# Two middle groups of 256 features made one of 512 in the first GEMM of a hybrid decoder layer

## The chip, the cores and the metric

The kernel runs on one core of one Trainium2 chip. The metric is the device time of one launch in microseconds (us). All inputs lie in HBM and the result is written to HBM.

## The reference, cut to what matters

One decoder layer: the input x (512 tokens, 2048 features, float32) is normalised, scaled and shifted by a conditioning vector, and multiplied by a wide matrix w_in. Behind it come a convolution branch, an attention branch, gates and two more projections, none of which the change touches.

```python
c_act = jax.nn.silu(c)                                   # (1, 2048)
mod = c_act @ w_ada + b_ada                              # w_ada: 2048 x 6144
shift, scale, gate = jnp.split(mod, 3, axis=-1)
h = rms_norm(x, g_pre) * (1.0 + scale) + shift           # 512 x 2048
p = h @ w_in                                             # w_in: 2048 x 11264
cv, cg, cz, q, k, v, az, m_conv, m_attn = split(p)       # cv, cg: 1024 columns each
u = cv * sigmoid(cg)
```

The columns of `mod` are dot products over all 2048 entries of c_act. A feature of h can therefore be formed only when its whole column of shift and its whole column of scale have been read, 2 x 2048 float32 numbers of w_ada per feature.

## The kernel before

**Precision.** Every float32 operand of a large product is split into two float32r parts, hi and lo (`split`, lines 141 to 151: the cast hi on ScalarE at line 145, the rest lo = src - hi on VectorE at line 146). A product is then three matmuls, hi*hi, hi*lo, lo*hi (`mm3`, line 167), each with a moving operand of 512 tokens.

**The first GEMM** computes cv and cg, 2048 output columns, which are 16 blocks of 128. It is the only product that runs while h is still being made. The 2048 features of h, the contraction, are 16 tiles of 128 (index k), and they are taken in the groups of `GROUPS`. An entry is (first feature, width, npe). For each group two generators exist:

- `ada(c0, width, npe)`, lines 287 to 339, makes h for the group. It loads w_ada in chunks of 512 KB (two DMAs of 256 KB on SP's queue, line 281, into a ring of AR = 6 buffers, tile `ada`). There are 16 steps kk, one for each 128 rows of w_ada. Of these, npe go to TensorE: two matmuls each (shift and scale) into 32 rows of a PSUM bank, tile `pa`, line 302, so that the matmuls of two such steps use four different column strips of the array. The others go to VectorE, one multiply-add over both halves, tile `acc`, lines 305 and 307. At the end the sums over 128 partitions are taken by matmuls with one or two output columns (tile `pm`). Where npe is 16, one matmul for each block of 128 features does it (line 318). Where npe is 0, two per block (line 324). Where npe lies between, four per block (lines 323 and 324), after VectorE has copied `pa` to `accp` (line 314). Three small VectorE operations give shift and scale, tiles `sh` and `scl` (lines 328 to 330). ScalarE then forms h (`hf`, line 335), and h is split into `hp`.
- `conv_gemm(k0, nk)`, lines 348 to 377, multiplies the nk tiles of the group by w_in. With nk = 2 it works in four steps of four output blocks, with nk = 4 in eight steps of two output blocks. Each step loads weights in blocks of 512 KB (`wr_c`, line 155, three buffers), splits them (`wh_c`, `wl_c`) and accumulates in PSUM tiles `pc` (four banks). For the first group ScalarE copies the results to `part` (line 367). For every later group VectorE adds each of the 16 PSUM tiles to its `part` (line 369). After the last group, `part` becomes u (lines 375 to 377).

**Order.** Lines 398 to 408 join the conv_gemm of group i with the ada of group i + 1, in program order, in proportion 4 or 8 steps of the one to `ST[i]` steps of the other:

```python
for i, (c0, width, _) in enumerate(GROUPS[:-1]):
    k0, nk = c0 // P, width // P
    conv, group = conv_gemm(k0, nk), ada(*GROUPS[i + 1])
    ...
    interleave((conv, 8 if nk == 4 else 4), (group, ST[i]), *([(rest, 8)] if i == 0 else []))
...
interleave((conv_gemm(KT - 4, 4), 8))
```

A step counts as issued when its share is the smallest. The compiler's planner then orders the instructions of each engine by this program order and by its own estimate of when each is ready. Each engine and SP's queue runs its list strictly in order.

Before the change the seven groups are 128, 128, 256, 256, 256, 512 and 512 features wide. The group that starts at 512 has all 16 sums on TensorE, that at 768 all on VectorE, that at 1024 half on each, and that at 1536 all on VectorE. After the first GEMM come v, q, k, attention, the gates and the projections.

Of the kernel before, what the change touches and what calls it, by code (L numbers as in the profile page):

```python
# [41 lines left out]
SKIP = 4  # L42
RES = 8
AR = 6
ST = (3, 10, 10, 10, 13, 10)

GROUPS = ((0, 128, 16), (128, 128, 16), (256, 256, 0), (512, 256, 16), (768, 256, 0),
          (1024, 512, 8), (1536, 512, 0))


@with_exitstack
def hybrid_trunk(ctx: ExitStack, tc: tile.TileContext, x, c, w_ada, b_ada, g_pre, g_post, w_in,
# [17 lines left out]
    def page(name, dt=F32):  # L70
        return pp.tile([P, S], dt, tag="pg", name=name)
# [105 lines left out]
    def interleave(*gens):  # L177

        gens = [[g, n, 0] for g, n in gens]
        while gens:  # L180
            g = min(gens, key=lambda e: (e[2] + 1) / e[1])
            g[2] += 1
            if next(g[0], StopIteration) is StopIteration:
                gens.remove(g)


    with tc.tile_pool(name="ps0", bufs=1, space=PSUM) as ps0, tc.tile_pool(name="ap", bufs=1) as ap:
# [70 lines left out]
        def norm_x(ks):  # L258
            for k in ks:
                nc.vector.tensor_tensor(xn[k], pxt[k], rsb, op=ALU.mult)  # L260

        def turn_norm(ks):
            for k in ks:
                turn((k,), range(NT))
                norm_x((k,))
                yield
# [81 lines left out]
        def conv_gemm(k0, nk):  # L348
            first, last = k0 == 0, k0 + nk == KT
            wk = min(nk, 4)  # L350
            nf = min(4, 8 // wk)
            for g in range(8 // nf):
                for a, c0 in ((0, C_CV), (1, C_CG)):
                    ps = [gbank(f"pc_{k0}_{g}_{a}_{f}") for f in range(nf)]
                    for q0 in range(k0, k0 + nk, wk):
                        key = (q0, g, a)
                        whi, wlo = early.pop(key) if key in early else conv_wsplit(q0, wk, g, nf, a, c0)
                        for f in range(nf):
                            fs = slice(f * P, (f + 1) * P)
                            for k in range(wk):  # L360
                                last_mm[0] = mm3(ps[f], (whi[:, k, fs], wlo[:, k, fs]), h[q0 + k],
                                                 q0 + k == k0, q0 + k == k0 + nk - 1)
                    for f in range(nf):
                        i = a * 8 + g * nf + f
                        if first:
                            part[i] = page(f"part_{i}")
                            nc.scalar.copy(part[i], ps[f])
                        else:
                            nc.vector.tensor_tensor(part[i], ps[f], part[i], op=ALU.add)  # L369
                    yield  # L370
                if last:
                    for f in range(nf):
                        i = g * nf + f
                        th = part[8 + i]
                        nc.scalar.activation(th, th, AF.Tanh, scale=0.5)
                        u[i] = page(f"u_{i}")
                        nc.vector.scalar_tensor_tensor(u[i], th, 1.0, part[i], op0=ALU.add, op1=ALU.mult)

        with tc.manual_schedule(engines={mybir.EngineType.PE, mybir.EngineType.Activation, mybir.EngineType.DVE}):
# [6 lines left out]
            norm_x(range(4))  # L386
            group = ada(*GROUPS[0])
            next(group)
# [8 lines left out]
        rest = turn_norm(range(8, KT))  # L397
# [3 lines that stand above are left out]
            if i == 0:  # L401
# [3 lines left out]
                with tc.issue_after(last_mm[0].ins):  # L405
                    for _ in range(2):
                        next(group)
            interleave((conv, 8 if nk == 4 else 4), (group, ST[i]), *([(rest, 8)] if i == 0 else []))
        cwrow = page("cwrow")
# [862 lines left out]
```

## Time and profile before

| what | us |
|---|---|
| median of 3 runs | 1429.47 |
| the 3 runs | 1425.40, 1429.47, 1429.83 |
| the profiled execution, its own time | 1427.9 |
| its span in the profile | 1426.1 |
| around the span (1427.9 - 1426.1) | 1.8 |

All rows below come from the profiled execution. Times in them are us from the start of the span unless marked ns. PE is TensorE, PEld its weight loads, DVE VectorE, ACT ScalarE, SP the queue that issues the transfers. An x behind a name is a number of recorded instructions. A float32 matmul, as in `pa` and `pm`, leaves two records, a float32r matmul one. An arrow and a name behind an idle time tell what ended it.

### The profile page before, as it was taken

To read this page: it belongs to the slowest core of one execution; us is meant where nothing else is said; L and a number is where in the kernel's file an instruction comes from. 1 tells how busy PE (TensorE), PEld (TensorE's weight loads), DVE (VectorE), ACT (ScalarE), POOL (GpSimd) and SP (SyncE) were. 2 spreads that over 40 slices of the span, in tenths; PEclk is the share of its full clock that TensorE was granted. 3 is DMA by queue.
4 is the path that set the end of the run, shared out by engine and by line. 5 is a ranking of instruction groups with operands and counts; after the bars stand their busy time and mean duration, and the time that the engine had idled before them with its cause. 6 is when DMAs were issued, how large, how long until landed. Compare 5 with 4: busy or idle time off the path is not lost.

```text
span 1426.1 us, 20678 instructions
## 1 busy us (share of the span) xinstructions
PE 1379.1 (97%) x7903; PEld 1171.8 (82%) x7903; DVE 1158.4 (81%) x1882; ACT 560.9 (39%) x907; POOL 59.6 (4%) x103
## 2 busy tenths in 40 slices
PE   5999999999999999999999999999999999989995
PEld 4676788887767877788999999999998888868784
DVE  6997975988888887588997788898966848897876
ACT  3421332223343244434544444444445313344443
POOL 0000000000000000000000000111000211010000
PEclk9999999999999999999999999999999999999998
DMA  9889733331322422233545556756569855546588
GB/s 300 288 285 308 232 117 102 118 130 63 102 83 69 131 67 82 74 126 134 200 161 188 176 171 193 255 196 200 171 204 345 301 182 194 198 122 211 171 238 262
DMA packets 178757, 254.89 MB, mean 179 GB/s; under 512 B 10065, under 2 KB 120994, under 8 KB 178274
## 3 DMA queue, kind: packets, MB, share of 16 engines
q1 hardware_dynamic: 169778, 227.61, 48.0%
q0 software_dynamic: 8880, 25.96, 6.9%
q8 instruction: 62, 1.02, 0.3%
q14 instruction: 37, 0.30, 0.1%
HBM read 221.29 MB, written 30.15 MB: 176 GB/s over the span
## 4 chain that ended last, share of the span: by engine, by line
PE 81%; DVE 10%; DMA 4%; issue 2%; ACT 2%; SPq 1%; DVEq 0%; ACTq 0%
PE pc L167 11%; PE py_ya L167 6%; PE pv L167 6%; PE pg_k L167 6%; PE pg_az L167 5%; PE pg_q L167 5%; PE x_ma L167 5%; PE x_mc L167 5%; PE z_mc L167 3%; PE z_ma L167 3%; PE y_ma L167 3%; PE y_mc L167 3%; PE x_cz L167 2%; PE oy L167 2%; DMA ga<-scratch_mc 2%
## 5 line engine op out<-in xcount | busy, mean ns | idle before, releaser
L500 DVE SCALAR_TENSOR_TENSOR cacc<-u,cw,cacc 128x511 f32<-128x511 f32 (+14 forms) x240 | 164.5, 729 | 0.0
L167 PE MATMUL pc<-hp,wh_c 128*128 128x512 f32 x512 | 160.2, 398 | 3.1 <-DVE part L369 1.2
L167 PEld LDWEIGHTS pc<-hp,wh_c 128*128 128x128 f32 x512 | 95.9, 190 | 29.1 <-issue 2.7
L167 PE MATMUL pc<-hp,wl_c 128*128 128x512 f32 x256 | 99.3, 397 | 2.1 <-DVE wl_c L146 2.1
L369 DVE TENSOR_TENSOR part<-pc,part 128x512 f32<-128x512 f32 x96 | 64.8, 688 | 25.3 <-PE pc L167 24.8
L167 PE MATMUL pv<-wh_v,hp 128*128 128x512 f32 x256 | 82.9, 398 | 0.9 <-DVE part L369 0.9
L167 PE MATMUL pg_q<-hp,wh_q 128*128 128x512 f32 x256 | 82.7, 399 | 0.0
L167 PE MATMUL pg_az<-hp,wh_az 128*128 128x512 f32 x256 | 81.5, 396 | 0.0
L167 PE MATMUL pg_k<-hp,wh_k 128*128 128x512 f32 x256 | 80.2, 393 | 0.0
L167 PE MATMUL py_ya<-ya,wh_ya 128*128 128x512 f32 x256 | 78.9, 390 | 0.0
L145 ACT CAST wh_c<-wr_c 128x1024 fp32r<-128x1024 f32 (+1 forms) x36 | 34.2, 956 | 104.1 <-PE pc L167 45.2
L167 PEld LDWEIGHTS pc<-hp,wl_c 128*128 128x128 f32 x256 | 48.5, 190 | 14.1 <-DVE wl_c L146 3.3
L167 PEld LDWEIGHTS pv<-wh_v,hp 128*128 128x128 f32 x256 | 47.8, 188 | 14.2 <-issue 4.5
L167 PEld LDWEIGHTS pg_az<-hp,wh_az 128*128 128x128 f32 x256 | 47.8, 188 | 11.9 <-issue 2.7
L167 PEld LDWEIGHTS pg_q<-hp,wh_q 128*128 128x128 f32 x256 | 47.3, 188 | 12.3 <-issue 2.8
L167 PEld LDWEIGHTS py_ya<-ya,wh_ya 128*128 128x128 f32 x256 | 48.0, 188 | 9.8
L652 POOL DMA_DIRECT2D adag<-in_w_ada_dram x64 | 34.2, 537 | 516.1 <-ACT oh L145 309.4
L167 PEld LDWEIGHTS pg_k<-hp,wh_k 128*128 128x128 f32 x256 | 48.0, 188 | 9.4
L307 DVE SCALAR_TENSOR_TENSOR acc<-ada,cact,acc 128x512 f32<-128x512 f32 (+1 forms) x52 | 50.5, 972 | 1.6 <-DMA ada<-in_w_ada_dram 1.4
L167 PE MATMUL py_yc<-ych,wh_yc 128*128 128x512 f32 x128 | 50.8, 397 | 0.3 <-DVE ga L957 0.3
L167 PE MATMUL pg_k<-hp,wl_k 128*128 128x512 f32 x128 | 51.1, 399 | 0.0
L167 PE MATMUL pv<-wl_v,hp 128*128 128x512 f32 x128 | 50.6, 396 | 0.0
(413 smaller groups left out, 3997.6 us busy)
## 6 DMA issues: line engine op xcount, KB each, us to landing
ada<-in_w_ada_dram SPq DMA_DIRECT2D x128, 256.0 KB, 5.4
wr_ma<-in_w_in_dram SPq DMA_DIRECT2D x16, 1024.0 KB
wr_mc<-in_w_in_dram SPq DMA_DIRECT2D x16, 1024.0 KB, 5.3
adag<-in_w_ada_dram POOLq DMA_DIRECT2D x64, 256.0 KB, 4.5
wr_c<-in_w_in_dram SPq DMA_DIRECT2D x28, 512.0 KB, 6.0
wr_v<-in_w_in_dram SPq DMA_DIRECT2D x8, 1024.0 KB, 6.8
wr_q<-in_w_in_dram SPq DMA_DIRECT2D x8, 1024.0 KB, 5.0
wr_k<-in_w_in_dram SPq DMA_DIRECT2D x8, 1024.0 KB, 5.3
```

The source lines that it names most:

```text
L145: nc.scalar.copy(hi, src)
L167: mm = nc.tensor.matmul(ps, a[p], b[q], start=start and i == 0, stop=stop and i == 2, skip_group_check=more)
L307: nc.vector.scalar_tensor_tensor(acc, raw[:, kk - k0, :, :], cact[:, kk:kk + 1], acc, op0=ALU.mult, op1=ALU.add)
L369: nc.vector.tensor_tensor(part[i], ps[f], part[i], op=ALU.add)
L500: paced(nc.vector.scalar_tensor_tensor(cvo[t][:, s:], u[t][:, :S - s], wj, cvo[t][:, s:], op0=ALU.mult, op1=ALU.add))
L652: nc.gpsimd.dma_start(out=raws[k], in_=ada_v[:, k, 2 * D + n * 512:2 * D + (n + 1) * 512])
```

## The change

Only constants change. The groups that start at 512 and 768 become one group of 512 features with npe = 8. `ST` loses an entry, and the group behind the first 256-wide one gets 13.

```diff
-ST = (3, 10, 10, 10, 13, 10)
-
-GROUPS = ((0, 128, 16), (128, 128, 16), (256, 256, 0), (512, 256, 16), (768, 256, 0),
-          (1024, 512, 8), (1536, 512, 0))
+ST = (3, 10, 13, 13, 10)
+
+GROUPS = ((0, 128, 16), (128, 128, 16), (256, 256, 0), (512, 512, 8), (1024, 512, 8), (1536, 512, 0))
```

The joins become: conv_gemm(128..255) with ada(256..511) as before; conv_gemm(256..511) with ada(512..1023), 4 steps to 13; conv_gemm(512..1023) with ada(1024..1535), 8 steps to 13; conv_gemm(1024..1535) with ada(1536..2047), 8 to 10 as before.

## Rows read from the trace of the kernel before

**Rows 1.** The page, span and part 1: busy us (share of the span) and instructions.

```profile
span 1426.1 us, 20678 instructions
PE 1379.1 (97%) x7903; PEld 1171.8 (82%) x7903; DVE 1158.4 (81%) x1882; ACT 560.9 (39%) x907; POOL 59.6 (4%) x103
```

**Rows 2.** The page, part 4: the chain that ended last, by engine.

```profile
PE 81%; DVE 10%; DMA 4%; issue 2%; ACT 2%; SPq 1%; DVEq 0%; ACTq 0%
```

**Rows 3.** Windows: length, busy us per engine (instructions), TensorE clock, DMA share, GB/s.

```profile
57.00:67.20 10.20, 8.23 (x65) 4.29 (x63) 9.64 (x19) 3.47 (x5) 0.00 (x0) 1.00 0.91 283
...
67.20:91.60 24.40, 24.40 (x123) 18.92 (x123) 22.04 (x35) 6.79 (x9) 0.00 (x0) 1.00 0.96 327
91.60:114.50 22.90, 22.90 (x106) 18.76 (x104) 21.62 (x35) 6.83 (x9) 0.00 (x0) 1.00 0.71 222
114.50:151.60 37.10, 36.51 (x161) 25.15 (x161) 26.66 (x37) 8.95 (x13) 0.00 (x0) 0.91 0.81 279
151.60:198.90 47.30, 46.00 (x211) 37.85 (x210) 42.28 (x53) 12.87 (x16) 0.00 (x0) 1.00 0.67 217
```

**Rows 4.** Timeline of PE at the edges of the stretch: start, us, work [idle before].

```profile
64.08 2.37 PE L302 MATMUL pa<-ada,c 128*32 128x256 f32 x40
...
67.28 1.45 PE L167 MATMUL pc<-hp,wh_c 128*128 128x512 f32 x5
...
151.60 1.97 PE L167 MATMUL pc<-hp,wh_c 128*128 128x512 f32 x8
154.88 0.50 PE L167 MATMUL pc<-hp,wl_c 128*128 128x512 f32 x1 [1.30 <-DVE wl_c L146]
```

**Rows 5.** The chain of waits, 67 to 110: sums of the two middle groups.

```profile
78.49 0.99 PE pa L302 x14
...
85.19 0.57 PE pa L302 x8
...
86.89 0.34 PE pm L318 x4
...
108.70 0.79 PE pm L324 x8
```

**Rows 6.** Groups on PE, 60 to 155, kept apart by shape: sums on TensorE.

```profile
L302 PE MATMUL pa<-ada,c 128*32 128x512 f32 x32 | 7.2, 603 | 0.6 <-DMA ada<-in_w_ada_dram 0.6
...
L302 PE MATMUL pa<-ada,c 128*32 128x256 f32 x64 | 4.7, 384 | 0.3 <-DMA ada<-in_w_ada_dram 0.3
```

**Rows 7.** Timeline of PE, 114 to 126: sums of the group at 1024.

```profile
114.55 1.91 PE L302 MATMUL pa<-ada,c 128*32 128x512 f32 x12
...
124.92 1.05 PE L302 MATMUL pa<-ada,c 128*32 128x512 f32 x2 [0.59 <-DMA ada<-in_w_ada_dram]
```

**Rows 8.** The chain of waits, 136 to 141: two of the sixteen pieces of `pm`.

```profile
136.67 0.22 PE pm L324 x2
...
138.90 0.40 PE pm L324 x2
```

**Rows 9.** Windows of PE alone: length, busy us (instructions), granted clock, DMA share, GB/s.

```profile
138.60:141.00 2.40, 2.40 (x14) 0.54 1.08 370
141.00:145.00 4.00, 4.00 (x11) 0.50 0.38 129
...
191.20:193.10 1.90, 1.90 (x19) 1.00 0.24 84
```

**Rows 10.** Timeline of DVE behind the sums of the group at 1024.

```profile
142.29 0.15 DVE L330 TENSOR_TENSOR scl<-scl,vec 128x4 f32<-128x4 f32 x1
...
148.75 1.29 DVE L146 TENSOR_TENSOR hp<-hf,hp 128x512 fp32r<-128x512 f32 x2
```

**Rows 11.** Groups on DVE, 60 to 155, kept apart by shape.

```profile
L369 DVE TENSOR_TENSOR part<-pc,part 128x512 f32<-128x512 f32 x54 | 36.2, 687 | 7.7 <-PE pc L167 7.5
...
L307 DVE SCALAR_TENSOR_TENSOR acc<-ada,cact,acc 128x512 f32<-128x512 f32 x17 | 12.7, 745 | 0.0
L307 DVE SCALAR_TENSOR_TENSOR acc<-ada,cact,acc 128x1024 f32<-128x1024 f32 x9 | 11.5, 1280 | 0.3 <-DMA ada<-in_w_ada_dram 0.3
```

## The prediction

> **What bounds the kernel now.** I first read the page's engine shares: PE is busy 1379.1 of 1426.1 us, DVE 1158.4 [rows 1]. The chain that ended last puts 81% on PE and 10% on DVE [rows 2]. Both are averages, so I cut the first GEMM into windows at the first matmul of each group of features [rows 3]. The group at 256 runs from 67.2 to 91.6, that at 512 to 114.5, that at 768 to 151.6, that at 1024 to 198.9. In the first two PE is busy without a break (24.40 of 24.40, 22.90 of 22.90). DVE is close behind (22.04, 21.62), and DMA moves 327 GB/s in the first. The third is the odd one: 37.10 us for the same 96 matmuls, PE busy 36.51, mean granted clock 0.91. So in the stretch that the change rebuilds, 67.28 to 151.60 [rows 4], PE sets the pace, DVE has some slack, and a microsecond that PE's list gains or loses there moves everything behind it.
>
> One group has 96 matmuls. In the second window they share 22.90 us with 0.79 us of `pm` [rows 3, 5]: about 0.23 us each, 22.1 us a group. The three groups' 288 matmuls, 66 us, stay. Only what lies between them changes.
>
> **The change part by part.**
>
> *Additions to `part`.* One group fewer means 16 fewer additions: 16 x 0.687 = 11.0 us less on DVE [rows 11]. On PE nothing goes, since PE did not wait for DVE from 67.2 to 114.5. What may go is one wait of 1.30 us for `wl_c` at 154.88 [rows 4].
>
> *Sums on VectorE.* 16 steps of 0.745 us become 8 of 1.280: 11.9 against 10.2, 1.7 us less on DVE [rows 11]. That is hidden like the additions. Together DVE loses about 12.7 us.
>
> *Sums on TensorE.* "Half" is no news in amount: before, one of the two groups had all sums on TensorE, the other none. 64 records of 256 columns become 32 of 512. But 64 took 4.7 us and the 32 of the group at 1024 took 7.2 us [rows 6]: with 512 columns, a step is issued as its chunk lands, often alone, and two strips of the array stay empty. The 64 were also well placed. 42 of them ran from 64.08 to 67.28, where PE waited for the next h [rows 4]. Only 14 and 8, 0.99 + 0.57 us, stood between matmuls [rows 5]. In the new group the ring of six buffers holds six steps, of which three are for TensorE. I let these three fall into the same wait, and give them the 1.9 us that three took at 114.55 [rows 7]. The other five steps stand on the path: 7.2 - 1.9 = 5.3 us. Added 5.3, removed 1.6. Bounds for the five: 2.5 us, if they pair up so that four strips fill (half of about 1.0 us each), and 7.2, if none finds the wait.
>
> *Sums over partitions.* The two old groups had 2 and 4 matmuls here (0.34 and 0.79 us [rows 5]). The new one has 16, as the group at 1024 has. These took 0.22 us each at full clock [rows 8]: 16 x 0.22 = 3.5 us. Added 3.5, removed 1.1.
>
> The Trainium skill's "TensorEngine Tiling (Array Packing)", section Performance Considerations, says that a one-column matmul costs about 60 cycles, as much as one of 60 columns. At 2.4 GHz that is an estimate of 25 ns each, 0.4 us in all, and the sum would end 3.1 us lower. The row with 0.22 us speaks against it, so the sum keeps the row.
>
> *The clock.* The group at 1024 had the same 16 matmuls in one block, and its clock fell to the lower of its two levels, 1.2 GHz, in the middle of it and stayed there to 145.0 at least [rows 9]. PE was never idle in it (2.40 of 2.40). Five matmuls of `pm` slowed from 0.22 to 0.40 us [rows 8], which cost 0.9 us. At least 4.0 us of large matmuls then ran at half rate, which cost 2.0 or a little more. One fall: 3.0 us. A block half as long, at 191.2, kept 1.00 [rows 9]. The new kernel has two such blocks of 16. I take a fall in both: one more than before, +3.0. Bounds: no fall in either (-3.0, since the old one goes too) and +3.0.
>
> *The wait for h.* Four tiles of h must be ready when the matmuls of the group at 256 run out. Behind `scl` at 142.29 the last `hp` ended at 150.04 [rows 10]: 7.7 us. The group reads 8.4 MB of w_ada. With six of sixteen chunks loaded ahead, 5.3 MB and 1.0 MB of weights are left at 67.2, 19 us at 327 GB/s: 86.5. Add 2 us for the last step and the copy, 3.5 for `pm`, 0.5 for `sh` and `scl`, and 7.7: about 100. PE's own work, 22.1 + 5.3 + 3.5, ends at 98.2 without a fall and at 101.2 with one. So with the fall I cost this wait at nothing: the slow matmuls cover it. Without that cover it is 2 us. Bounds 0 and 6: 6 if half of DVE's eight steps (5.1 us) and the copy behind them are still to do when the last chunk has landed, for DVE has 10.2 us of them in a stretch in which it was busy 90% with less [rows 3].
>
> *Idle time that goes.* The 0.59 us wait for w_ada [rows 7] goes, since the group at 1024 now has 44 us of matmuls to load behind instead of 22. So does the 1.30 us for `wl_c`. -1.9, bounds 0 and -1.9.
>
> *Queues.* The bytes and the number of transfers on SP's queue are the same. Rows of w_ada grow from 1 to 2 KB, rows of `wr_c` in this group shrink the other way. I cost that at nothing, bounds -1 and +1 us.
>
> Sum: -1.6 + 5.3 - 1.1 + 3.5 + 3.0 - 1.9 = +7.2 us. Against the profiled execution's own 1427.9 that is 1435.1. The median of the runs shown is 1429.47, 1.6 above that execution, so the median may come out as much higher.
>
> **The rivals.**
>
> *DVE sets the pace, and the change is faster.* Place: the two windows in which DVE is busy 90% and 94% [rows 3]. If PE's list only looks full there because matmuls are spread to what DVE delivers, the 12.7 us come back less the 6.1 of added PE work. That is 1421, with no fall of the clock 1418. It decides if PE's own work from 67.3 on is shorter than what DVE has in the same time. Against it: 96 matmuls at 0.23 us fill the second window by themselves. Chance 0.12.
>
> *No clock fall, and the work fits.* Sixteen short matmuls among longer stretches of matmuls keep the clock in both blocks: 7.2 - 3.0 - 3.0 = +1.2 us, with the 2 us wait for h +3.2. That is 1429 to 1431, no change. A fall in one of the two gives 4.2, on the edge. For it: the second block now stands behind 44 us of dense matmuls. Against it: it is the block itself in which the clock fell. Chance 0.27. The Trainium skill's "TensorE: Matmul & The Clock Gate", section Why this matters for your kernels, ties drops to idle gaps between bursts. By that rule neither block falls. The row with PE busy 2.40 of 2.40 at clock 0.54 does not agree.
>
> *h comes late.* w_ada or DVE's eight steps delay h by the 6 us above, PE stands idle and the clock falls as well: +13 us, 1441. For it: DMA is at 0.96 there, and the new group asks for twice the bytes in front of one group of 256. Chance 0.11.
>
> *The change does nothing.* The planner could spread the new group's matmuls so that PE's list costs what it cost. As every piece is fixed in number, this is the second rival's case.
>
> **How the numbers follow.** Forecast 0.50 (1431 to 1439 by itself: one fall more or none, and the pairing of the sums), no change 0.27, late h 0.11, faster 0.12. About 0.3% (4.3 us) is what a measurement of this kernel can tell from no change. Slower by more: 0.50 + 0.11 = 0.61; within: 0.27; faster: 0.12. The range leaves out the faster rival and the far end of the late h: 1427 to 1442.
>
> **What would show each step.** Right: `part` with 80 additions instead of 96; `pa` of 512 columns with 64 records and about 14 us; two blocks of `pm` with 32 records each, around 90 to 100 and around 150; the granted clock at 0.5 behind both; the first matmul of the group at 1024 some 7 us after 151.60; the rest of the kernel shifted by the same. Wrong: the clock at 1.00 around 95 (the first fall missing), PE idle before the group at 512 with an arrow to `hp` (late h), or PE's stretch shorter than 84 us (DVE was the pace).

## The result, and the profile after

The changed kernel took 1436.07 us, the median of 4 runs (1435.47 to 1438.98), beside 1428.57 us for the kernel before in the same comparison. The ratio is 1.0061, with a 95% interval of 1.0042 to 1.0080: slower by about 7.5 us, which is more than the 0.3% bound of the prediction. The forecast was 1435.1 us in a range of 1427 to 1442. The profiled execution took 1436.53 us, 8.6 us more than the profiled one of before (1427.9).

The page's span, engine shares and the group of additions, to be read against [rows 1] and [rows 11]:

```profile
span 1434.8 us, 20625 instructions
...
PE 1388.6 (97%) x7891; PEld 1173.5 (82%) x7891; DVE 1148.1 (80%) x1855; ACT 561.5 (39%) x907; POOL 59.8 (4%) x103
...
L368 DVE TENSOR_TENSOR part<-pc,part 128x512 f32<-128x512 f32 x80 | 54.1, 689 | 40.4 <-PE pc L166 40.1
```

The change did what its text says. There are 80 additions in place of 96, and DVE's busy time fell by 10.3 us. PE's rose by 9.5 us. The time followed PE.

The windows of the kernel after are cut at the same events as [rows 3]: the first matmul of the group at 256 (68.61), of the group at 1024 (160.4), of the group at 1536, of v (250.88). Columns as there.

```profile
68.60:160.40 91.80, 91.61 (x406) 64.73 (x406) 66.77 (x83) 21.71 (x29) 0.00 (x0) 0.96 0.82 275
160.40:205.90 45.50, 45.50 (x210) 37.69 (x208) 34.75 (x46) 12.68 (x16) 0.00 (x0) 1.00 0.56 179
205.90:250.80 44.90, 44.10 (x195) 36.11 (x194) 26.61 (x36) 14.27 (x18) 0.00 (x0) 1.00 0.33 106
250.80:1434.80 1184.00, 1160.28 (x6762) 1000.55 (x6762) 967.02 (x1562) 484.04 (x793) 57.96 (x95) 0.99 0.51 166
```

The same view of the kernel before, for the whole of the rebuilt stretch and for all that follows the first v matmul:

```profile
67.20:151.60 84.40, 83.81 (x387) 62.84 (x387) 70.31 (x104) 22.57 (x30) 0.00 (x0) 0.96 0.83 277
243.70:1426.10 1182.40, 1158.43 (x6762) 1000.00 (x6762) 967.35 (x1562) 483.34 (x793) 57.81 (x95) 1.00 0.51 166
```

The loss is in the rebuilt stretch: 91.8 us for 84.4, and PE has no idle time in it to speak of (91.61 of 91.80). Its start is 1.3 us later than before, the two windows behind it are 1.7 us shorter together (90.4 for 92.1), and the rest of the kernel is 1.6 us longer with the same 6762 matmuls. That last piece lies in one place. In windows of all engines, the profiled execution of the kernel after has a fall of the clock around 1276 us, and that of before has none at the same work:

```profile
1276.00:1280.00 4.00, 3.79 (x10) 3.00 (x11) 3.58 (x7) 2.08 (x3) 0.89 (x2) 0.57 0.30 83
```

```profile
1269.00:1273.00 4.00, 3.87 (x17) 3.18 (x18) 3.58 (x7) 3.04 (x4) 0.97 (x2) 1.00 0.31 91
```

What PE did in the stretch stands in the chain of waits: start, us, what.

```profile
75.53 1.04 PE pa L301 x2
76.57 2.04 PE pc L166 x8
78.62 0.98 PE pa L301 x2
79.59 0.89 PE pc L166 x3
80.49 0.97 PE pa L301 x2
...
84.64 0.98 PE pa L301 x4
...
92.21 0.22 PE pm L323 x2
...
95.33 0.22 PE pm L323 x2
...
107.63 0.99 PE pa L301 x8
...
142.17 0.22 PE pm L323 x2
```

A piece of `pa` between matmuls takes 0.97 to 1.04 us whether it holds one matmul (x2), two (x4) or four (x8). In the new group most go singly: the shift chunk and the scale chunk of a step come by different transfers, and each matmul is issued as its chunk lands. Both blocks of `pm` run at 0.22 us a matmul to the end. Each of these matmuls leaves two records, and in front of each record the profile has a weight load of 128 columns of its own: in the first block 32 loads and 32 records in 3.46 us, one every 0.11 us. So 0.22 us is also the pace of two such loads in a row; that the loads set it is likely, and no run here tries it. The groups on PE from 60 to 262, kept apart by shape, give the totals that answer to [rows 6]:

```profile
L301 PE MATMUL pa<-ada,c 128*32 128x512 f32 x64 | 16.4, 605 | 1.5 <-DMA ada<-in_w_ada_dram 1.5
...
L322 PE MATMUL pm<-halves,accp 128*128 128x1 f32 x32 | 5.6, 245 | 0.0
```

PE's timeline at the edges of the stretch shows the late start: the third step that was to fall into the wait for h comes with a wait of its own for w_ada, and its x4 takes 1.69 us.

```profile
66.99 1.69 PE L301 MATMUL pa<-ada,c 128*32 128x512 f32 x4 [1.29 <-DMA ada<-in_w_ada_dram]
68.61 0.73 PE L166 MATMUL pc<-hp,wh_c 128*128 128x512 f32 x2
...
250.88 0.47 PE L166 MATMUL pv<-wh_v,hp 128*128 128x512 f32 x1 [0.88 <-DVE part L368]
```

The granted clock behind the two blocks, in windows of PE alone (columns as in [rows 9]):

```profile
95.50:98.90 3.40, 3.40 (x9) 0.51 0.92 321
98.90:102.00 3.10, 3.10 (x12) 1.00 0.02 6
143.00:146.50 3.50, 3.50 (x10) 0.53 1.07 380
146.50:150.00 3.50, 3.50 (x17) 0.98 1.07 369
```

and the one fall of the kernel before, in the same view:

```profile
138.60:145.30 6.70, 6.70 (x24) 0.52 0.64 217
```

Two falls instead of one, as forecast, but each begins where its block ends and lasts 3.4 to 3.5 us, while the single fall of before began inside its block and lasted 6.7 us.

### The profile page after: what moved, and what is told of

Its sections match the earlier page's. It is cut to its first block, busy times and chain, and to the rows that moved or that the text cites. A ratio compares the mean times of both kernels' runs of the same rounds, so it can differ in the third digit from the quotient of the medians.

```text
span 1434.8 us, 20625 instructions
## 1 busy us (share of the span) xinstructions
PE 1388.6 (97%) x7891; PEld 1173.5 (82%) x7891; DVE 1148.1 (80%) x1855; ACT 561.5 (39%) x907; POOL 59.8 (4%) x103
## 4 chain that ended last, share of the span: by engine, by line
PE 80%; DVE 11%; DMA 5%; issue 2%; ACT 2%; SPq 0%; DVEq 0%; ACTq 0%
PE pc L166 11%; PE py_ya L166 6%; PE pv L166 6%; PE pg_k L166 6%; PE pg_az L166 5%; PE pg_q L166 5%; PE x_ma L166 5%; PE x_mc L166 5%; PE z_ma L166 3%; PE z_mc L166 3%; PE y_ma L166 3%; PE y_mc L166 3%; DMA ga<-scratch_mc 2%; PE oy L166 2%; PE x_cz L166 2%
## 5 line engine op out<-in xcount | busy, mean ns | idle before, releaser
L368 DVE TENSOR_TENSOR part<-pc,part 128x512 f32<-128x512 f32 x80 | 54.1, 689 | 40.4 <-PE pc L166 40.1
L166 PE MATMUL pg_az<-hp,wl_az 128*128 128x512 f32 x128 | 50.6, 396 | 0.0
```

What stands on the lines that cost most here:

```text
L166: mm = nc.tensor.matmul(ps, a[p], b[q], start=start and i == 0, stop=stop and i == 2, skip_group_check=more)
```

## The experiments

All edits are against the changed kernel unless a line says otherwise. The theory (A): PE's list in the stretch sets the time, and the time is lost in sums that are issued singly and in the second block of sixteen one-column matmuls. The main rival (B): DVE, the transfers or the wait for h, or the merging itself, set it. A third (C), for two of the runs: the proportion in which the two instruction lists are joined (`ST`).

**All sums of the new group on TensorE.**

```diff
-... (512, 512, 8), ...
+... (512, 512, 16), ...
```

> The merged group has all 16 sums on TensorE instead of 8. Theory A (what the new group puts into TensorE's list between the large matmuls sets the time: about 7 us of 512-column sums, 3.5 us of one-column matmuls, and a clock at half for some 3 us behind them): eight more steps of up to 1 us each (+4 to +8), but only 4 two-column matmuls in place of 16 (-2.6) and no half clock behind them (-1.7): 1436 to 1440, and the clock stays at 1.00 around 95 us. Theory B (VectorE's share of the sums makes h late): VectorE loses some 10 us in front of the new group, the time falls to 1430 to 1433.

It took 1434.06 us, ratio 1.0038 [1.0024, 1.0052]: 2 us less than the changed kernel by the medians, with intervals that overlap, and between what A and B expected. The groups on PE, 60 to 262:

```profile
L301 PE MATMUL pa<-ada,c 128*32 128x512 f32 x96 | 19.9, 601 | 0.0
```

and windows of PE:

```profile
94.00:98.00 4.00, 4.00 (x19) 1.00 0.57 173
134.00:138.00 4.00, 4.00 (x16) 0.58 0.69 246
```

Half as many sums again cost only 3.5 us more (19.9 for 16.4). With every step on TensorE, neighbouring chunks are both for PE, and more of the matmuls share the array. `pm` of this group shrinks from 16 matmuls to four of two columns, and the first fall is gone. The one that is left begins inside its block, and at 138 to 140 us the clock is still at 0.50. The expectation had scaled the sums by their number, which is wrong: what counts is how many pieces they are issued in.

**All sums of the new group on VectorE.**

```diff
-... (512, 512, 8), ...
+... (512, 512, 0), ...
```

> The merged group has all 16 sums on VectorE instead of 8. Theory A: TensorE's list loses about 7 us of sums and a wait of 1.3 us, 8 one-column matmuls instead of 16 (-1.8), no half clock (-1.7), some -11 us in all, of which VectorE's 16 steps of 1.28 us may give back up to 10 as a wait for h, since they do not fit into 30 us beside its additions and splits: 1425 to 1435, with the group's own stretch of TensorE idle before the first matmul of the new group. Theory B (VectorE makes h late): ten more us there, 1442 to 1447.

1439.07 us, ratio 1.0071 [1.0055, 1.0088], between the two expectations. The window of the stretch in which the group's h is made, with all engines:

```profile
68.00:101.00 33.00, 26.02 (x103) 18.50 (x101) 30.37 (x35) 3.60 (x4) 0.00 (x0) 0.86 0.89 291
```

and the waits of PE, 60 to 105 (in total, times, longest):

```profile
PE pc L166 <- DVE part L368: 3.8, 5, 1.1
PE pc L166 <- DVE wl_c L145: 3.7, 3, 1.6
PE pc L166 <- ACT hp L144: 2.7, 1, 2.7
```

Here DVE is the pace: 30.37 us busy of 33.0, and PE idle for 7, waiting for `part` and `wl_c`. (The wait for `hp` ends at 67.02, in front of the group at 256. It is the one that the sums on PE fill in the other kernels.) The run is no faster for the sums that PE is rid of. So DVE has room in the changed kernel, but less than those eight steps take (8 x 1.28 = 10 us).

**DVE's gain put back.** Sixteen additions' worth of work that changes no value, in two of the groups.

```diff
+                            if k0 in (2, 4) and i % 2:
+                                nc.vector.tensor_tensor(part[i], part[i], part[i], op=ALU.max)
```

> The changed kernel with 16 operations of about 0.6 us put back on VectorE (each takes a part against itself), 8 behind the products of the group at 256 and 8 behind those of the group at 512, in place of the 16 additions that the change removed. Theory A (VectorE has slack there and the removed additions were worth nothing): 1436, +0 to +1.5. Theory B (VectorE's 11 us were worth something, and other costs hide it): +4 to +10, 1440 to 1446.

1437.64 us, ratio 1.0064 [1.0042, 1.0087], beside 1.0061 for the changed kernel. The groups on DVE:

```profile
L370 DVE TENSOR_TENSOR part<-part 128x512 f32<-128x512 f32 x16 | 10.9, 684 | 0.0
```

10.9 us more on DVE leave the time where it was, as far as 4 runs between 1433.5 and 1441.5 can tell. So the additions that the change removes were worth nothing that can be measured, as forecast, and most of B's 4 to 10 us is ruled out. The profiled execution is the slowest of the four, 5.0 us longer than that of the changed kernel. Of that, 2.3 us stand in front of the group at 256, before any of the added operations, where PE waits 3.40 us for w_ada. Behind it the clock is low for longer (two falls of some 6.8 us, from 93.5 and from 144.7, where the changed kernel has 3.4).

**The sums four at a time.** In groups of 512 with sums on both engines, two steps are collected and their four matmuls issued back to back, the one that waits for the last chunk first.

```diff
-            n = 0
+            n, quad = 0, []
...
-                    if on_pe:
+                    if on_pe and width == 512 and npe < KT:
+                        quad += [(kk, n, a, raw, k0) for a in range(2)]
+                        if len(quad) == 4:
+                            first = None
+                            for kq, nq, a, rq, kq0 in reversed(quad):
+                                m = 2 * a + nq % 2
+                                with tc.issue_after(first.ins) if first is not None else nullcontext():
+                                    mm = nc.tensor.matmul(pa[32 * m:32 * m + 32, :width], c32[:, kq, :],
+                                                          rq[:, kq - kq0, a, :], start=nq < 2, stop=nq >= npe - 2)
+                                first = first if first is not None else mm
+                            quad = []
+                    elif on_pe:
```

> In both groups with half their sums on TensorE, four matmuls (two steps) are issued back to back once the last of their chunks has landed, so that they use four strips at once. Same matmuls, same transfers. Theory A: each four costs 1.0 us instead of 1 us for each one or two, so about 4 us a group in place of about 7 and 6: -4 to -5 us, 1431 to 1432. Theory B (transfers and VectorE decide when h is ready): no change, 1436, or slower because buffers are held longer, up to 1439.

1432.85 us, ratio 1.0032 [1.0020, 1.0044]: 3.2 us less than the changed kernel. The groups on PE, 60 to 170:

```profile
L305 PE MATMUL pa<-ada,c 128*32 128x512 f32 x64 | 8.5, 605 | 0.0
```

The same 64 records take 8.5 us for 16.4. Not all of the 7.9 us come back, and the windows of PE show a part of why:

```profile
64.00:68.00 4.00, 2.46 (x19) 1.00 0.85 269
68.00:72.00 4.00, 3.84 (x10) 0.57 0.96 335
90.00:94.00 4.00, 4.00 (x31) 0.79 1.06 393
94.00:98.00 4.00, 4.00 (x13) 0.50 0.94 331
```

A part of the sums had stood in the wait for h at 64 to 68, where they cost nothing. With fewer there, PE idles for 1.71 us before the group's first matmul (1.29 in the changed kernel, whose clock was 1.00 from 68 to 72), and this time the clock fell behind that too. The same holds in all the profiled executions of this document: in the seven in which PE idled 1.71 to 3.40 us at that place the clock fell there, in the seven in which it idled 0 to 1.43 us it did not.

The Trainium skill, "TensorEngine Tiling (Array Packing)", section Tiling Modes, says that different tiles of the array can load weights and multiply in parallel. The pieces of 0.97 to 1.06 us with one, two or four matmuls agree with it.

**Twelve `pm` matmuls for sixteen.** The sums from TensorE (`accp`) for shift and scale of a block in one matmul of two columns.

```diff
+                if npe:
+                    nc.tensor.matmul(pm[:, 2 * b:2 * b + 2], accp[:, bs], halves, start=True, stop=False,
+                                     skip_group_check=True)
...
-                    if npe:
-                        nc.tensor.matmul(col, accp[:, bs], halves[:, a:a + 1], start=True, stop=False)
-                    nc.tensor.matmul(col, acc[:, a, bs], ones[:, :1], start=not npe, stop=True)
+                    nc.tensor.matmul(col, acc[:, a, bs], ones[:, :1], start=not npe, stop=True,
+                                     skip_group_check=bool(npe))
```

> In both groups with half their sums on TensorE the sums over partitions take 12 matmuls instead of 16 (shift and scale of the TensorE part in one matmul of two columns). Theory A: 4 x 0.22 us less in each of two blocks, -1.8 us, 1434; if the shorter block of 2.7 us no longer lets the clock fall, another -1.7 to -3.5: 1431 to 1433. Theory B: no change, 1436.

1432.52 us, ratio 1.0036 [1.0022, 1.0049]: 3.6 us less. Eight matmuls at 0.22 us are 1.8 of it. Windows of PE behind the two blocks:

```profile
94.00:98.00 4.00, 4.00 (x21) 1.00 1.05 374
...
142.00:146.00 4.00, 4.00 (x20) 1.00 1.07 374
```

In the profiled execution, one of the fastest, neither fall is there. The eight runs lie between 1430.6 and 1437.4 with mean clocks of 0.989 to 0.996, so the falls are not gone from every execution. Nor are they gone with twelve as such: in the profiled executions of the four kernels below that have blocks of twelve, the clock fell behind five of six. That the other 1.8 us come from the clock is therefore likely, and not shown.

**Every `pm` matmul of the mixed groups twice.**

```diff
-                for a in range(2):
+                for a in [a for a in range(2) for _ in range(2 if npe else 1)]:
```

> The changed kernel with every one-column matmul for the sums over partitions of its two groups of 512 with half their sums on TensorE issued twice (32 instead of 16 in each of two blocks; the second writes the same sums again). Theory A (they stand on the path): 2 x 16 x 0.22 = +7.0 us, and the longer block keeps the clock at half for longer, another 0 to +4: 1443 to 1447. Theory B (they stand in a wait for h or in other slack): up to +2, 1436 to 1438.

1450.54 us, ratio 1.0161 [1.0140, 1.0182]: 14 us more than the changed kernel. The chain of waits, in the two blocks:

```profile
94.87 0.22 PE pm L323 x2
...
99.59 0.43 PE pm L323 x2
...
147.05 0.22 PE pm L322 x2
...
150.10 0.43 PE pm L322 x2
```

and the clock behind the first:

```profile
98.00:102.00 4.00, 4.00 (x17) 0.50 0.01 4
102.00:106.00 4.00, 4.00 (x11) 0.50 0.00 2
```

The 32 added matmuls are 7.0 us at 0.22 (two blocks of sixteen). In each block the clock falls part of the way through, so that the rest of it runs at 0.43. The second block takes 10.3 us for the 3.5 of the changed kernel, the first 9.2. This prices the block: under B it would have cost next to nothing. The expectation of A was too low because it did not let the blocks themselves slow down.

**Both cures: fours and twelve.** The edits of the two runs together.

> The changed kernel with both cures: sums on TensorE in fours, and 12 instead of 16 matmuls for the sums over partitions, in both groups with half their sums on TensorE. Theory A (TensorE's list): the two effects lie in different places of the list and add up, -4 from the fours and -2 to -5 from the shorter blocks: 1427 to 1430, level with the kernel before. Theory B (the merging itself is slow, since h comes in one piece of four tiles): no lower than the better of the two alone, 1432 to 1433.

1428.54 us, ratio 0.9998 [0.9987, 1.0009]. The two gains add up, and the loss is gone as far as the interval can tell. So the way in which sums and `pm` are issued on PE is enough to explain the size of it. It does not say that the merged groups are as good as the old ones, since both cures also shorten the group at 1024. That needs the next run.

**Both cures on the kernel before.** There they touch the group at 1024 alone.

> The kernel before with both cures, which touch only its group at 1024. Theory A: its sums on TensorE fall from about 7 to 4 us, of which some stood in a wait (-1 to -3), 4 matmuls fewer (-0.9), and its one fall of the clock goes in most runs (-1 to -3): 1422 to 1426. Theory B: that group is bound by transfers (DMA share above 0.9 there), no change, 1428.

1424.84 us, ratio 0.9978 [0.9969, 0.9987]: the fastest of all, and the only one here whose interval lies below 1. The groups on PE:

```profile
L306 PE MATMUL pa<-ada,c 128*32 128x512 f32 x32 | 4.3, 604 | 2.6 <-DMA ada<-in_w_ada_dram 2.6
```

7.2 us have become 4.3, and `pm` has lost four matmuls. With the same cures the merged kernel is 3.7 us behind (1428.54 for 1424.84). About 3.0 of that can be counted in the chains: the new group has three pieces of sums on the path (1.12 + 1.06 + 0.99 = 3.2 us) and twelve `pm` matmuls (2.6), where the two old groups have 1.6 and 1.1. In the two profiled executions the first v matmul is only 0.2 us apart (242.84 and 242.66), but in its execution the cured kernel before had waited 4.5 us for w_ada (1.9 and 2.6), so the difference of the medians can't be placed row by row.

**The two groups of 256 not merged, but half on each engine** (against the kernel before).

```diff
-... (512, 256, 16), (768, 256, 0),
+... (512, 256, 8), (768, 256, 8),
```

> The kernel before with half the sums on each engine in both groups of 256 (8 and 8 steps), but no merging. It has 16 one-column matmuls for the sums over partitions here instead of 6, in two blocks of 8. Theory A: 10 x 0.22 = +2.2 us, the clock stays (blocks of 1.8 us), the 256-column sums cost about what they cost: 1429 to 1432. Theory B (what costs is the engines' sharing of a group's sums, whose results must meet before h): as slow as the merged kernel, 1435 to 1437.

1439.27 us, ratio 1.0080 [1.0066, 1.0095], 7 us above the upper end of A and 2 above that of B. The groups on PE, 60 to 170:

```profile
L302 PE MATMUL pa<-ada,c 128*32 128x512 f32 x32 | 9.7, 603 | 0.0
L302 PE MATMUL pa<-ada,c 128*32 128x256 f32 x64 | 8.2, 399 | 2.0 <-DMA ada<-in_w_ada_dram 2.0
```

`pa` takes 17.9 us for the 11.9 of [rows 6], with the same number of records of each shape. In the chain of waits `pm` takes 6.9 for 5.6, and a wait of 2.0 us for w_ada (0.3 before) stands in front, as in the changed kernel. That is 9.0 us of the 9.8 us by which its first v matmul is later. I had expected the 256-wide sums to keep the price of [rows 6]. But that price belonged to a group that had all of its steps on TensorE. Split in halves, every second step is for the other engine, and the pieces go out singly. So the split costs without the merging, as much as both together do in the changed kernel (1.0080 beside 1.0061, with intervals that overlap). The edit also changes how the group at 1024 is laid out (9.7 for 7.2), so the two effects are not separate here.

**The order share.**

```diff
-ST = (3, 10, 13, 13, 10)
+ST = (3, 10, 10, 13, 10)
```

> The changed kernel with the share of the new group's steps at 10 instead of 13 for four steps of products, so that its last steps stand later in the program order. Theory A: the same matmuls stand in TensorE's list, 1434 to 1437. Theory C (13 puts the new group's work too early, in front of matmuls that could run): the wait in front of the group at 256 and some single sums go, 1430 to 1433.

1433.25 us, ratio 1.0040 [1.0025, 1.0055], about 2.8 us less than the changed kernel by the medians, with intervals that overlap. The groups on PE, 60 to 170:

```profile
L301 PE MATMUL pa<-ada,c 128*32 128x512 f32 x64 | 13.7, 605 | 1.4 <-DMA ada<-in_w_ada_dram 1.4
```

Later in the order, more chunks have landed when their turn comes, and the sums pair up by themselves: 13.7 us for 16.4. The wait in front of the group at 256 that C expected to go is still there (1.43 us). In this profiled execution the first fall of the clock is missing as well, though its block still has sixteen matmuls (90.65 to 94.11, clock 1.00 until 133.3). So C may have a share in the loss, through the same sums, but the time alone does not establish it.

**Order share on top of both cures**, to see if it adds anything where the sums go in fours anyway.

> The kernel with fours and 12 matmuls (1428.5) and the share of the new group's steps at 10 instead of 13, which alone gained 3 us. Theory A: that gain came from sums that no longer stood alone and from a wait for one of them, which the fours have already removed: 1427 to 1430, no further gain. Theory C (the earlier place in the order is itself a cost): another -3, 1425 to 1426.

1426.97 us, ratio 0.9992 [0.9982, 1.0003]. This lies at A's lower edge. Its interval overlaps that of the two cures alone, so a gain of its own is not established.

**All on TensorE, in fours**, the first edit with both cures.

> All 16 sums of the merged group on TensorE, in fours, and 12 matmuls for the sums over partitions of the group at 1024. Against the run with all sums on TensorE (1434.1, where they took some 13 us in pieces), theory A: eight fours of 1.0 us, -4 to -5; the group at 1024 in fours, -2; four matmuls less, -0.9 and at times a fall of the clock: 1425 to 1427, level with or below the kernel before. Theory B (VectorE's slack decides, and that is used up by the other groups): no lower than the same kernel with half the sums on VectorE, 1428.5 to 1430.

1427.28 us, ratio 0.9988 [0.9975, 1.0001]. The groups on PE, 60 to 170:

```profile
L305 PE MATMUL pa<-ada,c 128*32 128x512 f32 x96 | 12.6, 603 | 0.4 <-DMA ada<-in_w_ada_dram 0.4
```

Ninety-six records cost less here than 64 did in the changed kernel. It is the same as the kernel before within the measurement. It is 2.4 us behind the cured kernel before by the medians, 1.4 by the ratios, whose intervals overlap.

## Why the prediction was right, point by point

The direction, the place and the total were right: +7.2 forecast, +7.5 between the medians, +8.6 between the profiled executions. The terms were not all right, and that the total came so close is in part luck: the clock was charged 2.9 us too much, the sums of the new group 1.9 too little, and the rest came from places that the sum did not hold. In us, from the two profiles:

| term | forecast | measured |
|---|---|---|
| sums of the new group on the path with their wait of 0.20 us, less the old 1.6 | +3.7 | +5.6 (7.2 - 1.6) |
| its three steps in the wait for h: from the first of them to the first matmul of the group at 256 | 0 | +0.8 (3.97 for 3.20) |
| sums of the group at 1024, with the 0.59 us wait | -0.6 | -1.5 (5.9 for 7.4) |
| `pm` at full clock | +2.4 | +2.2 (6.9 for 4.7) |
| clock, by the windows above: length times what is missing to 1.00 | +3.0 | +0.1 (3.3 for 3.2) |
| `wl_c` wait and the rest to the first v matmul | -1.3 | -1.7 |
| the rest of the stretch | 0 | +0.9 |
| group at 256 late before its sums | 0 | +0.6 |
| behind the first v matmul: a fall of the clock | 0 | +1.6 |
| sum | +7.2 | +8.6 |

**What sets the pace.** Right. PE is busy 91.61 of 91.80 us. DVE, 11.0 + 1.7 us lighter by the sum, gave nothing back, and putting 10.9 us on it again cost nothing measurable. The faster rival had DVE as the pace and falls with that. The run with all sums on DVE shows where it would have begun to hold.

**Sums on TensorE: the mis-sized term.** The forecast took 5.3 us for the five steps on the path, and 7.2 as the bound "if none finds the wait". Three did find the wait, and the five alone still took 7.2, in seven pieces. The step that failed is the price by step. 7.2 us for eight steps [rows 6] was an average over a group whose steps partly paired up (the x12 piece of [rows 7] beside its x2). What is paid is a piece, about 1.0 us, however many of the four strips it fills, and the new group issued its last steps in singles. The same rule explains why the group at 1024 became cheaper: behind 44 us of matmuls more of its chunks had landed, three of its six pieces are x8, and its wait of 0.59 us is gone, as forecast. The run in fours shows the price by piece: 16.4 us became 8.5.

**`pm`.** Right: 0.22 us each, and 16 of them in 3.47 us. The Trainium skill's figure ("TensorEngine Tiling (Array Packing)", section Performance Considerations), an estimate of 0.4 us for all, falls. The run with every `pm` doubled lost 14 us, where an estimate from that figure (32 matmuls of 25 ns) is 0.8.

**The clock: right mechanism, wrong size.** There are two falls for one, both behind a block of one-column matmuls in which PE was busy throughout. But the forecast charged each with 3.0 us, the price of the old one. Each of the new ones came at the end of its block and lasted half as long, 1.7 us a fall. The block was thought to fix where the clock falls, and it does not: the same sixteen matmuls of the group at 1024 had the fall in the middle before and at the end after. Nor is a fall sure: behind eleven of the twelve blocks of sixteen in the profiled executions here the clock fell, behind one (with the share at 10) it did not. The step that failed is taking one execution's fall for the price of every fall.

The Trainium skill, "TensorE: Matmul & The Clock Gate", section Why this matters for your kernels, puts drops down to idle gaps between bursts. The falls around 68 behind PE idling for 1.71 to 3.40 us agree in kind. The two falls behind the blocks, with PE busy 3.40 of 3.40 and 3.50 of 3.50, do not.

**The wait for h.** Right at nothing, with little to spare. The last `hp` of the new group on DVE, and on PE the first matmul of the group at 512:

```profile
103.45 1.28 DVE L145 TENSOR_TENSOR hp<-hf,hp 128x512 fp32r<-128x512 f32 x2
```

```profile
106.44 1.20 PE L166 MATMUL pc<-hp,wh_c 128*128 128x512 f32 x4
```

Forecast were about 100 and 101.2. Both came later, and h was ready 1.7 us before PE was, which is what the fall in front of it cost PE. Whether that cover was needed is not shown: in the run with the share at 10, where this fall is missing, PE did not wait for `hp` either. PE's idle time up to the group at 512 is one wait for w_ada of 0.20 us. The late-h rival did not come about. With all sums on DVE PE waits for other things of DVE's, not for the new group's `hp`.

**What was not in the sum.** The 1.29 us wait for w_ada in front of the group at 256 is one: a sum that fills a wait can also be later than the wait. The forecast's ring of six buffers was right, but the third step's chunk had not landed. Behind the first v matmul the same work took 1184.0 us for 1182.4, and the difference arises at the fall of the clock around 1276. In the profiled executions of all the kernels here that stretch lies between 1181.7 and 1186.9 us, in kernels with and without the merged group, so it is scatter between executions and no effect of the change. The 0.6 us before the group at 256's sums lies in work that the change does not touch: with the clock at 0.66 from 20 to 30 us, the transposes of x took 3.65 us for 3.26, and the last 0.2 us is not traced.

**What stays open.** Of the 3.7 us that the merged kernel is behind with both cures, 0.7 is not attributed, and the 3.0 are counted and not tried one by one. Nor is it known what decides whether the clock falls behind a block of twelve or sixteen.

## What to carry to other kernels

Price matmuls that use a part of the array by the piece in which they are issued, not by their number or size: work that is split between two engines step by step leaves each engine with lone pieces, and collecting them was worth more here than the split. Work taken from an engine that is not the pace gave nothing back, though the engine was busy 90% in the first part of the stretch. A row that averages a group (7.2 us for 32 records) is safe as a price only where the new pieces will be issued in the same company, so look at the single pieces in the chain first.

## What the runs showed of the hardware

- The granted clock fell to its lower level (1.2 GHz) behind blocks of one-column float32 matmuls with PE fully busy. The sixteen of the group at 1024 brought a fall that began in the block and lasted 6.7 us in one kernel, and one that began at its end and lasted 3.5 us in the other. Over all the profiled executions it fell behind eleven of twelve blocks of sixteen and behind five of eight blocks of twelve. With all doubled, the fall came inside both blocks.
- A matmul of 512 columns into 32 rows took 0.97 to 1.04 us alone, and four of them on four strips took 0.99 to 1.12 us together when issued back to back.
- A float32 matmul with one column took 0.22 us at the full clock, in step with its two weight loads of 128 columns.
- Where less work stood in the wait at 64 to 68, PE idled longer, and with idle times of 1.71 to 3.40 us the clock fell (0.57 from 68 to 72 in the run in fours). So filling a wait can be worth more than the time of the work.
